# Down stage of an MLP: operand splits tied to a later product, a second output buffer, the last two jobs added to x1 on chip

## The chip, the cores and the metric

The kernel runs on one core of a Trainium2 chip. The metric is the device time of one execution in microseconds (us), the median of several runs. PE does the matmuls, ACT, DVE and POOL do elementwise work, SP issues most of the DMA transfers, POOL some.

## The reference, cut to what matters

One layer (a gated linear recurrence, a sparse attention, their merge and output projection), then an MLP with squared ReLU and a final norm, over 1024 prompt tokens and 32 sample tokens (1056 in all), in float32. The model width is 1024, the MLP's is 4096. The change is in the MLP's second half and in what follows it; all before that stays as it is.

```python
def _rmsnorm(x, g):
    xf = x.astype(jnp.float32)
    y = xf * lax.rsqrt(jnp.mean(xf * xf, axis=-1, keepdims=True) + EPS) * g.astype(jnp.float32)
    return y.astype(x.dtype)
...
def _layer(x, s0, attend, lb, w_in, hg_norm, w_a, w_b, w_o, norm1, norm2, w_up, w_down):
...
    m = jax.nn.sigmoid(ga) * y_a + jax.nn.sigmoid(gb) * y_b
    x = x + m @ w_o
    h2 = _rmsnorm(x, norm2)
    x = x + jnp.square(jax.nn.relu(h2 @ w_up)) @ w_down
    return x, s_new, ak, av, ik
...
    y_prompt = _rmsnorm(xp, norm_f)
    y_sample = _rmsnorm(xs, norm_f)
```

## The kernel before, in words

Tokens lie along the free axis, 1056 of them in two halves of 528 (TH). Both matrix products of the MLP are done as a scheme that needs seven products for eight blocks, P1 to P7, the operands of which are sums and differences of blocks. Every product runs in three passes, high part times high part and twice high times low, so each operand is split into a rounded half, o[:, 0], and a remainder, o[:, 1].

The work is a list of 32 jobs, JOBS. Jobs 0 to 15 are "up" jobs (h2 @ w_up, squared ReLU); 14 of them (NPAIR) leave seven operands each in DRAM (hc_d, by combos and the rows near L1433), and the last two leave their hidden rows in hid_d. Jobs 16 to 31 are "down" jobs (times w_down) for four rounds r and four output columns m, each over k = 2, 3 or 4 pairs of hidden rows: k is 2, 3, 4, 4 in the first round, 4 in the second and third, and 4, 3, 2, 2 in the last. A product is two halves (c = 0, 1) of k times 3 matmuls of 128x264. SEVEN is the order of all products: P2, P6, P5, P7 of a job, P1 of the next, then P4 and P3. The scheduler that places instructions on the engines' queues may still move a ready instruction ahead; an engine then works through its queue in that order.

OPS holds four slots of seven operands each (tiles h2a, h2b, h2P). An operand of a new pair is loaded by SP (op_load, L1348) into the remainder half after the last product that reads the slot's old content. op_split then casts it on ACT (L1352) and subtracts on DVE (L1353). It is written two products after the load (late_ops). The new operand is read by the same product of the next job, seven products after the load. TAKE says which job's products load which pair: 14 pairs, 98 operands, in 10 of the jobs 15 to 27, four of these with two pairs.

After a product its PSUM result is evacuated: P1, P6 and P7 by ACT's copies uu (L1398), P4 of a down job by ACT (L1406), P2, P7 and P3 by DVE's adds into hd (L1400, L1402, L1408). The weights of coming products are summed by DVE (L1290) and split on ACT and DVE (L1302, L1303). hd[j] has two rows: e = 0 comes from y0, a ring of two buffers, and e = 1 from y1, a ring of one. After P4 and P3 of a down job POOL accumulates hd into x1_d in DRAM (L1440). After each of the last four jobs the two finished rows of x1 are read back (L1447). HD, the hidden rows of the last two up jobs, is loaded (L1451) and split (L1454, L1455). Then last_w loads four weight pieces through one buffer (L1373) and splits them (L1375, L1376), and down() multiplies them with HD over three chunks of tokens (pd, L156 to L158), adds to x1 on DVE (L1497), and final() transposes (yT, L1476), normalizes and stores.

## Time and profile before

| what | value |
|---|---|
| median of 3 runs | 1807.02 us (1801.29 to 1813.28) |
| the profiled execution | 1804.69 us, its span 1803.0 us |
| PE busy in the span | 1718.2 us (95%) |
| DVE, ACT, POOL busy | 1222.6, 867.4, 216.7 us |
| up jobs end, down jobs begin | at about 1400 us |
| last stage (pd, yT) begins | at about 1714 us |

The profiled execution lies 2.3 us under the median, and 1.7 us of it are outside of the span. A busy share is an average over the whole span; the rows further down are of single stretches.

### The profile page before, as it was taken

To read this page: it belongs to the slowest core of one execution; us is meant where nothing else is said; L and a number is where in the kernel's file an instruction comes from. 1 tells how busy PE (TensorE), PEld (TensorE's weight loads), DVE (VectorE), ACT (ScalarE), POOL (GpSimd) and SP (SyncE) were. 2 spreads that over 40 slices of the span, in tenths; PEclk is the share of its full clock that TensorE was granted. 3 is DMA by queue.
4 is the path that set the end of the run, shared out by engine and by line. 5 is a ranking of instruction groups with operands and counts; after the bars stand their busy time and mean duration, and the time that the engine had idled before them with its cause. 6 is when DMAs were issued, how large, how long until landed. Compare 5 with 4: busy or idle time off the path is not lost.

```text
span 1803.0 us, 30879 instructions
## 1 busy us (share of the span) xinstructions
PE 1718.2 (95%) x11980; PEld 1656.2 (92%) x11980; DVE 1222.6 (68%) x2767; ACT 867.4 (48%) x1645; POOL 216.7 (12%) x244
## 2 busy tenths in 40 slices
PE   6999999999999999979999999999999999999887
PEld 6999999999999998877899998999999899999867
DVE  7275585745799897965747569777677866566535
ACT  6456465334578833234724455444344644444412
POOL 1100000023000015740100230000000000000110
PEclk9999999999999999999999999999999999999998
DMA  5411111231223234552543243444334877676763
GB/s 167 132 49 48 49 56 48 61 94 34 84 68 96 77 95 130 172 180 66 162 143 108 95 132 99 145 151 160 132 132 156 275 178 182 174 185 166 171 155 115
DMA packets 162706, 221.92 MB, mean 123 GB/s; under 512 B 12096, under 2 KB 117856, under 8 KB 162560
## 3 DMA queue, kind: packets, MB, share of 16 engines
q1 hardware_dynamic: 137472, 148.60, 26.4%
q0 software_dynamic: 18032, 62.18, 13.4%
q10 hardware_dynamic: 7056, 9.18, 1.4%
q8 instruction: 94, 1.54, 0.4%
q14 instruction: 52, 0.43, 0.1%
HBM read 140.31 MB, written 76.77 MB: 120 GB/s over the span
## 4 chain that ended last, share of the span: by engine, by line
PE 38%; DMA 9%; issue 8%; DVE 4%; ACT 3%; POOL 2%; DVEq 0%; SPq 0%; POOLq 0%; ACTq 0%
PE pua L1336 13%; PE puc L1336 7%; PE pub L1336 3%; DMA qb<-q_d 2%; PE po L158 2%; PE po L157 2%; PE po L156 2%; DMA h2a<-hc_d 2%; DMA wdr<-in_w_down_dram 1%; POOL qb L924 1%; DMA h2b<-hc_d 1%; DMA wbsg<-sg_d 1%; DVE pr L923 1%; PE wbp L156 1%; PE wbp L157 1%
## 5 line engine op out<-in xcount | busy, mean ns | idle before, releaser
L1336 PE MATMUL pua<-h2P,wP 128*128 128x264 f32 x1248 | 196.1, 285 | 3.5 <-ACT uu L1398 3.1
L1336 PE MATMUL pua<-h2a,wP 128*128 128x264 f32 x960 | 161.7, 287 | 13.6 <-ACT uu L1398 10.6
L1336 PEld LDWEIGHTS pua<-h2P,wP 128*128 128x128 f32 x1248 | 170.4, 189 | 4.5 <-ACT uu L1398 4.0
L1336 PEld LDWEIGHTS pua<-h2a,wP 128*128 128x128 f32 x960 | 134.6, 189 | 18.9 <-ACT uu L1398 14.8
L1398 ACT COPY uu<-pua 128x264 f32<-128x264 f32 x192 | 72.0, 378 | 133.5 <-PE pua L1336 127.4
L156 PE MATMUL wgt<-hh,wgth 128*128 128x352 f32 x384 | 126.1, 328 | 0.0
L158 PE MATMUL wgt<-hh,wgtl 128*128 128x352 f32 x384 | 125.1, 326 | 0.0
L157 PE MATMUL wgt<-hl,wgth 128*128 128x352 f32 x384 | 124.6, 324 | 0.0
L1336 PE MATMUL pua<-h2b,wP 128*128 128x264 f32 x672 | 118.4, 285 | 0.0
L1336 PE MATMUL puc<-h2P,wP 128*128 128x264 f32 x720 | 111.0, 284 | 0.6 <-DVE hd L1402 0.6
L1440 POOL DMA_DIRECT2D x_d<-hd x32 | 27.9, 873 | 612.6 <-ACT wP L1302 359.5
L1336 PEld LDWEIGHTS puc<-h2P,wP 128*128 128x128 f32 x720 | 97.1, 188 | 0.8 <-DVE hd L1402 0.8
L777 ACT ACTIVATE jkA<-sc,bstg 128x1024 bf16<-128x1024 bf16 (+5 forms) x93 | 87.1, 936 | 21.3 <-DVE bstg L796 6.0
L1336 PEld LDWEIGHTS pua<-h2b,wP 128*128 128x128 f32 x672 | 96.8, 189 | 0.1
L772 DVE TENSOR_SCALAR_CACHE_REDUCE jkD<-sc,bstg 128x768 bf16<-128x768 f32 (+3 forms) x96 | 84.4, 879 | 0.9
L1303 DVE TENSOR_TENSOR wP<-w1r,wP 128x512 fp32r<-128x512 f32 (+2 forms) x96 | 62.8, 655 | 28.8 <-ACT wP L1302 28.0
L1302 ACT CAST wP<-w1r 128x512 fp32r<-128x512 f32 (+2 forms) x96 | 57.0, 595 | 46.7 <-PE puc L1336 28.1
L156 PEld LDWEIGHTS wgt<-hh,wgth 128*128 128x128 f32 x384 | 72.2, 188 | 2.0 <-issue 1.0
L157 PEld LDWEIGHTS wgt<-hl,wgth 128*128 128x128 f32 x384 | 72.2, 188 | 1.2 <-issue 0.5
L158 PEld LDWEIGHTS wgt<-hh,wgtl 128*128 128x128 f32 x384 | 72.2, 188 | 1.2 <-issue 0.6
L1336 PE MATMUL puc<-h2a,wP 128*128 128x264 f32 x384 | 70.6, 286 | 0.9 <-DVE hd L1408 0.9
L158 PE MATMUL po<-mh,wol 128*128 128x352 f32 x192 | 62.2, 324 | 0.0
(788 smaller groups left out, 5071.2 us busy)
## 6 DMA issues: line engine op xcount, KB each, us to landing
x_d<-hd POOLq DMA_DIRECT2D x32, 528.0 KB
hc_d<-hd SPq DMA_DIRECT2D x56, 264.0 KB, 2.8
h2P<-hc_d SPq DMA_DIRECT2D x45, 264.0 KB, 3.7
sg_d<-gst ACTq DMA_DIRECT2D x48, 176.0 KB, 2.0
h2a<-hc_d SPq DMA_DIRECT2D x32, 264.0 KB, 2.8
wgtr<-in_w_in_dram SPq DMA_DIRECT2D x16, 512.0 KB, 3.9
qb<-q_d POOLq DMA_DIRECT2D x16, 512.0 KB
w1r<-in_w_up_dram SPq DMA_DIRECT2D x16, 512.0 KB, 3.9
```

What stands on the lines that cost most here:

```text
L156: nc.tensor.matmul(ps, wh, xh, start=(k == 0), stop=False)
L157: nc.tensor.matmul(ps, wh, xl, start=False, stop=False)
L158: nc.tensor.matmul(ps, wl, xh, start=False, stop=(k == n - 1))
L772: nc.vector.tensor_scalar(jkD[:, 0, :L], SC[i], s if isinstance(s, float) else s[:, a:a + 1], 0.0, op0=op, op1=ALU.add, accum_out=out[:, a ...
L777: nc.scalar.activation(jkA[:, 0, :(i + 1) * 128], src(i), AF.Sign, bias=thr[:, a:a + 1], accum_out=cnt[:, a:a + 1])
L923: nc.vector.tensor_tensor(pr, kp[:, 0:1, :].to_broadcast([128, 2, 512]), qb, op=ALU.mult)
L924: nc.gpsimd.tensor_tensor(qb, kp[:, 1:2, :].to_broadcast([128, 2, 512]), qb, op=ALU.mult)
L1302: nc.scalar.copy(w[:, 0, :n], src)
L1303: nc.vector.tensor_tensor(w[:, 1, :n], src, w[:, 0, :n].bitcast(F32), op=ALU.subtract)
L1336: nc.tensor.matmul(ps, w[:, a, k], x[:, b, sl], start=(q in "P1P2P5" and k == n_ == 0), stop=(k == k1 - k0 - 1 and n_ == 2), skip_group_ch ...
L1398: nc.scalar.copy(uu[c][:, {"P1": u1, "P6": 1, "P7": 2}[q]], ps)
L1440: nc.gpsimd.dma_start(x1_d[2 * i + e], hd[j][e], accum_op=ALU.add)
```

## The change

It edits the loop over the products and op_split in five ways. The cast of a split becomes an ACTIVATE scaled by hold, a column of ones that a small TENSOR_SCALAR (ones_after) makes from the output of the product at which the split is written. The split is written four products after its load (five where the fourth is a P5, so that P4's and P3's come together at a P7). The tile tt, free after the 14th up job, becomes a second buffer of y1 until job NJ-3's P3. The jobs NJ-2 and NJ-1 add hd to x1 on chip with DVE; for that the x1 rows 4 to 7 are read by SP and 0 and 1 by POOL after job NJ-4, and 2 and 3 after NJ-3. And the splits of HD come after P3 of job NJ-2, four products later than before, tied in the same way by a column from DVE.

```diff
@@ -1349,7 +1349,7 @@
 
     def op_split(p, q):
         o = OPS[p % 4, q]
-        nc.scalar.copy(o[:, 0], o[:, 1].bitcast(F32))
+        nc.scalar.activation(o[:, 0], o[:, 1].bitcast(F32), AF.Copy, scale=hold)
         nc.vector.tensor_tensor(o[:, 1], o[:, 1].bitcast(F32), o[:, 0].bitcast(F32), op=ALU.subtract)
 
     def combos(i):
@@ -1384,6 +1384,13 @@
         rb_chunk(prb[:, c, :CH], slice(c * CH, (c + 1) * CH))
     LO, HI = slice(0, TH), slice(TH, T)
     late_ops = collections.defaultdict(list)
+    hold = None
+
+    def ones_after(eng, src):
+
+        one = sm.tile([128, 1], F32, name="one", tag="one", bufs=4)
+        eng.tensor_scalar(one, src, 1.0, 1.0, op0=ALU.max, op1=ALU.min)
+        return one
     for g, (j, q) in enumerate(SEVEN):
         kind, i, k0, k1 = JOBS[j]
         if q == "P2":
@@ -1417,12 +1424,15 @@
             if p + 2 < NJ:
                 w_raw(p + 2, h)
 
+        if g in late_ops:
+            hold = ones_after(nc.gpsimd, uu[1][:, {"P1": u1, "P6": 1, "P7": 2}[q], 0:1] if q in ("P1", "P6", "P7") else
+                              hd[j][{"P2": 0, "P4": 1, "P3": 0}[q]][:, (T if q == "P3" else TH) - 1:][:, :1])
         for p, q_ in late_ops.pop(g, ()):
             op_split(p, q_)
         for p in range(NPAIR):
             if TAKE[p] == j:
                 op_load(p, q)
-                late_ops[g + 2].append((p, q))
+                late_ops[g + 4 + (SEVEN[g + 4][1] == "P5")].append((p, q))
         if kind == "up":
             if q in ("P2", "P7", "P4", "P3"):
                 e, sl = {"P2": (0, LO), "P7": (1, HI), "P4": (1, LO), "P3": (0, HI)}[q]
@@ -1433,25 +1443,39 @@
                     nc.sync.dma_start(hc_d[i, ORDER.index({"P2": "P1", "P7": "P3", "P4": "P2"}[q])], hd[j][e][:, sl])
             if q == "P3" and i < NPAIR:
                 combos(i)
+            if (i, q) == (NPAIR - 1, "P3"):
+                U.put(tt)
+                y1.ids.append(U.free.pop())
             if (i, q) == (NU - 1, "P3"):
-                U.put(sqs, tt)
+                U.put(sqs)
+        elif j >= NJ - 2:
+
+            if q in ("P2", "P7", "P4", "P3"):
+                e, sl = {"P2": (0, LO), "P7": (1, HI), "P4": (1, LO), "P3": (0, HI)}[q]
+                x1 = X1[2 * i + e]
+                nc.vector.tensor_tensor(x1[:, sl], x1[:, sl], hd[j][e][:, sl], op=ALU.add)
         elif q in ("P4", "P3"):
             e = int(q == "P4")
             nc.gpsimd.dma_start(x1_d[2 * i + e], hd[j][e], accum_op=ALU.add)
 
             if j >= NJ - 4 and q == "P3":
+                back = range(2 * i, 2 * i + 2)
                 if j == NJ - 4:
                     U.put(*(OPS[2, q_] for q_ in ORDER))
-                for e in range(2):
-                    X1[2 * i + e] = U.get([128, T], F32, f"x1_{2 * i + e}")
-                    nc.gpsimd.dma_start(X1[2 * i + e], x1_d[2 * i + e])
+                    back = (4, 5, 6, 7, 0, 1)
+                for m in back:
+                    X1[m] = U.get([128, T], F32, f"x1_{m}")
+                    (nc.sync if m >= 4 else nc.gpsimd).dma_start(X1[m], x1_d[m])
                 if j == NJ - 3:
                     HD = [tuple(h2b[:, 4 * a + e].rearrange("p a t -> p (a t)") for a in range(2)) for e in range(4)]
                     for e in range(4):
                         nc.sync.dma_start(HD[e][1].bitcast(F32), hid_d[e])
-        if g == len(SEVEN) - 11:
+                    U.free.append(y1.ids.pop())
+                    y1.i = 0
+        if g == len(SEVEN) - 7:
+            hold = ones_after(nc.vector, hd[j][0][:, T - 1:T])
             for hi, lo in HD:
-                nc.scalar.copy(hi, lo.bitcast(F32))
+                nc.scalar.activation(hi, lo.bitcast(F32), AF.Copy, scale=hold)
                 nc.vector.tensor_tensor(lo, lo.bitcast(F32), hi.bitcast(F32), op=ALU.subtract)
         if g == len(SEVEN) - 6:
             r0.close()
```

On ACT, where the last two operands of the pair loaded during job 21 are split, P4's and P3's: h2b is that pair's slot, wP a split weight, pua the PSUM of P1, P6, P7 and P4, hd1 the second output row. Before:

```order
L1352 CAST h2b_10251<-h2b_10251 128x528 [waits DMAHW2_49]
L1398 COPY uu_10292<-pua_15456 128x264 [waits DVE_49,PE_49]
L1406 COPY hd1_15317<-pua_15215 128x264 [waits PE_49]
L1302 CAST wP1_15516<-w0r_15245 128x512
L1398 COPY uu_10293<-pua_15456 128x264 [waits DVE_49,PE_49]
L1302 CAST wP2_15618<-w1r_15350 128x512 [waits DMAHW7_49,Activation_49]
L1352 CAST h2b_10251<-h2b_10251 128x528 [waits DMAHW4_49]
L1302 CAST wP6_15650<-ws_10294 128x512 [waits PE_49,Activation_49]
L1398 COPY uu_10292<-pua_15686 128x264 [waits PE_49]
L1398 COPY uu_10292<-pua_15456 128x264 [waits PE_49]
```

Now, at the same two operands (one is the column of ones):

```order
L1302 CAST wP2_15686<-w1r_15402 128x512 [waits DMAHW6_49,PE_49,Activation_49]
L1405 COPY uu_10293<-pua_15758 128x264 [waits PE_49]
L1302 CAST wP5_15748<-ws_10294 128x512 [waits DVE_49]
L1405 COPY uu_10293<-pua_15514 128x264 [waits PE_49]
L1302 CAST wP6_15716<-ws_10294 128x512
L1302 CAST wP3_15882<-w1r_15402 128x512 [waits DVE_49,PE_49,Activation_49]
L1405 COPY uu_10292<-pua_15514 128x264 [waits PE_49]
L1405 COPY uu_10293<-pua_15514 128x264 [waits PE_49]
L1302 CAST wP7_15785<-w0r_15291 128x512
L1352 ACTIVATE h2b_10251<-h2b_10251,one_15752 128x528 [waits DMAHW3_49,Pool_49]
L1352 ACTIVATE h2b_10251<-h2b_10251,one_15752 128x528 [waits DMAHW1_49]
L1413 COPY hd1_15621<-pua_15514 128x264 [waits DMASW4_49,PE_49]
```

Both splits now stand behind the copies of P7 and wait for the column as well as the load. Before, they stood some rows apart, the second ahead of three copies uu, and waited for the load alone.

On PE, at P4 of a job whose P4 takes operands of two new pairs (h2a and h2P4 in the wP4 rows), the order before, from P4's first half on:

```order
L1336 MATMUL pua_14964<-h2P4_10007,wP4_15063 128x264 [waits Activation_49]
L1336 MATMUL pua_14964<-h2P4_10007,wP4_15063 128x264 x2
L1336 MATMUL pua_14964<-h2b_10251,wP4_15063 128x264 x3
L1336 MATMUL pua_14964<-h2a_9339,wP4_15063 128x264 x3
L1336 MATMUL pua_14964<-h2P4_9766,wP4_15063 128x264 x3
L1336 MATMUL puc_15148<-h2P3_10008,wP3_15101 128x264 [waits DVE_49]
L1336 MATMUL puc_15148<-h2P3_10008,wP3_15101 128x264 x2
```

Now, from six matmuls behind P7's last on:

```order
L1336 MATMUL pua_15261<-h2b_10251,wP1_15059 128x264 [waits Activation_49]
L1336 MATMUL pua_15261<-h2b_10251,wP1_15059 128x264 x2
L1336 MATMUL pua_15261<-h2a_9339,wP1_15059 128x264 x6
L1336 MATMUL pua_15261<-h2P1_10002,wP1_15059 128x264 x3
L1336 MATMUL pua_14994<-h2P4_10007,wP4_15097 128x264 [waits Activation_49]
L1336 MATMUL pua_14994<-h2P4_10007,wP4_15097 128x264 x2
L1336 MATMUL pua_14994<-h2b_10251,wP4_15097 128x264 x3
L1336 MATMUL puc_15188<-h2P3_10008,wP3_15139 128x264 [waits DVE_49]
L1336 MATMUL puc_15188<-h2P3_10008,wP3_15139 128x264 x2
L1336 MATMUL puc_15188<-h2b_10251,wP3_15139 128x264 x3
L1336 MATMUL pua_14994<-h2a_9339,wP4_15097 128x264 [waits Activation_49]
L1336 MATMUL pua_14994<-h2a_9339,wP4_15097 128x264 [waits DVE_49]
```

P4's first half is begun with the two old operands, products P1 and P3 run before and behind that, and the first matmul with a new operand (wP4 with h2a) waits for ACT, the one after it for DVE. 30 matmuls lie between P7's last and it. Before, all four operands of P4 were read in a row.

On POOL, in job 23, which takes two pairs, and the start of job 24 (x1_d is x1 in DRAM), the queue before held the accumulating transfers alone; now:

```order
L1392 TENSOR_SCALAR one_15920<-uu_10293 128x1 [waits Activation_49,Pool_49]
L1392 TENSOR_SCALAR one_16026<-uu_10293 128x1 [waits Activation_49,Pool_49]
L1459 DMA x1_d_9335<-hd0_15852 128x1056 [waits DMASW2_49,DVE_49]
L1392 TENSOR_SCALAR one_16062<-hd1_15853 128x1 [waits Activation_49,Pool_49]
L1459 DMA x1_d_9335<-hd1_15853 128x1056 [waits DMASW3_49]
L1392 TENSOR_SCALAR one_16100<-hd0_15852 128x1 [waits Pool_49]
L1392 TENSOR_SCALAR one_16145<-hd0_16109 128x1 [waits DVE_49,Pool_49]
L1392 TENSOR_SCALAR one_16182<-uu_10293 128x1 [waits Activation_49,Pool_49]
```

Each column of ones (L1392) waits for an evacuation by ACT or DVE, and the transfers stand between them in the same queue.

## Rows read from the trace of the kernel before

**Rows 1.** Four stretches: length, busy time of each engine, granted clock, DMA share, GB/s.

```profile
1080.00:1400.00 320.00, 316.93 (x2576) 314.48 (x2575) 241.62 (x452) 141.65 (x284) 3.49 (x1) 1.00 0.42 141
1400.00:1436.00 36.00, 32.50 (x253) 31.03 (x252) 31.80 (x63) 25.77 (x58) 1.83 (x2) 1.00 0.85 290
1436.00:1700.00 264.00, 251.31 (x2025) 248.69 (x2024) 157.32 (x283) 122.37 (x258) 21.82 (x26) 0.99 0.69 174
1700.00:1803.00 103.00, 80.97 (x540) 73.85 (x538) 48.94 (x130) 28.25 (x78) 9.16 (x13) 0.92 0.53 148
```

**Rows 2.** What PE waited for, 1400 to 1803 us: total, times, longest.

```profile
PE pua L1336 <- ACT uu L1398: 11.7, 14, 2.0
PE yT L1476 <- DVE x L1497: 7.8, 2, 7.0
PE puc L1336 <- DVE hd L1402: 3.0, 2, 2.4
PE pd L156 <- DVE x L1497: 2.6, 2, 2.0
PE pua L1336 <- ACT wP L1302: 2.2, 2, 1.3
```

**Rows 3.** What ACT waited for at the operand cast, 1395 to 1803 us.

```profile
ACT h2b L1352 <- DMA h2b<-hc_d: 26.2, 11, 5.5
ACT h2a L1352 <- DMA h2a<-hc_d: 24.2, 16, 4.3
ACT h2P L1352 <- DMA h2P<-hc_d: 19.0, 13, 4.7
```

**Rows 4.** Timelines of SP, ACT, PE: start, duration, operation, idle time before.

```profile
1535.38 0.46 SPq L1348 DMA_DIRECT2D h2b<-hc_d  x1
...
1545.49 0.63 ACT L1352 CAST h2b<-h2b 128x528 fp32r<-128x528 f32 x1 [5.46 <-DMA h2b<-hc_d]
...
1546.97 1.18 PE L1336 MATMUL pua<-h2a,wP 128*128 128x264 f32 x6 [2.04 <-ACT uu L1398]
```

**Rows 5.** What DVE waited for, 1400 to 1803 us; then POOL's timeline.

```profile
DVE x L1497 <- DMA x<-x_d: 18.2, 3, 11.9
DVE hd L1402 <- DMA x_d<-hd: 14.0, 4, 5.4
...
1761.01 0.54 POOL L1447 DMA_DIRECT2D x<-x_d  x1 [7.24 <-DMA x_d<-hd]
```

**Rows 6.** Two stretches of the end, columns as in the first group.

```profile
1725.00:1750.00 25.00, 22.95 (x118) 19.26 (x117) 6.38 (x10) 3.60 (x7) 1.99 (x3) 0.93 0.58 137
1750.00:1775.00 25.00, 16.67 (x112) 15.59 (x111) 8.28 (x27) 4.17 (x15) 2.53 (x4) 0.86 0.48 125
```

**Rows 7.** Groups by line and shape: ns min/median/max, first and last start.

```profile
L1352 ACT CAST h2P<-h2P x45: 627/634/641, 1394.5 to 1676.7; 128x528 fp32r<-128x528 f32 x45
L1353 DVE TENSOR_TENSOR h2P<-h2P x45: 698/707/714, 1395.1 to 1677.3; 128x528 fp32r<-128x528 f32 x45
L1186 ACT CAST h2P<-x x10: 397/408/414, 1036.4 to 1060.6; 128x264 fp32r<-128x264 f32 x10
L1254 ACT ACTIVATE h<-x,g x4: 501/502/517, 1074.1 to 1080.9; 128x264 f32<-128x264 f32 x4
L1246 POOL TENSOR_TENSOR sqs<-sqs,sq x21: 937/1133/3488, 1001.4 to 1080.7; 128x352 f32<-128x352 f32 x21
```

**Rows 8.** ACT's timeline: the first and last cast of the last weights.

```profile
1713.01 1.05 ACT L1375 CAST wdh<-wdr 128x1024 fp32r<-128x1024 f32 x1 [0.69 <-DMA wdr<-in_w_down_dram]
...
1740.55 1.05 ACT L1375 CAST wdh<-wdr 128x1024 fp32r<-128x1024 f32 x1 [7.97 <-DMA wdr<-in_w_down_dram]
```

**Rows 9.** POOL's timeline, then DVE's, around 1081 us, ahead of the up jobs.

```profile
1080.71 3.49 POOL L1246 TENSOR_TENSOR sqs<-sqs,sq 128x352 f32<-128x352 f32 x1 [4.70 <-ACT sq L1245]
...
1082.95 0.43 DVE L1200 TENSOR_TENSOR tb<-h,ta 128x264 f32<-128x264 f32 x1
1084.23 0.43 DVE L1198 TENSOR_TENSOR ta<-x 128x264 f32<-128x264 f32 x1 [0.84 <-POOL sqs L1246]
```

## The prediction

> **What bounds the kernel now.** I read the table of stretches first [rows 1]. From 1080 to 1400 us, the up jobs, PE is busy 316.93 of 320.00 us at full clock: nothing is to be had there, and 2576 matmuls in that time give 0.123 us for one. What the change touches comes after 1400 us. In the transition to the down jobs (1400 to 1436) PE lacks 36.00 - 32.50 = 3.5 us while DVE is busy 31.80, which is 88%; in the other down jobs (1436 to 1700) it lacks 12.7 us; in the last stretch (1700 to 1803) 22.0 us, of which some 10 follow the last matmul and stay.
>
> The list of what PE waited for after 1400 us [rows 2] sums to 27.3 us. The largest is a wait for ACT's copies uu, 11.7 us in 14 pieces. ACT is not busy then: its own list [rows 3] says that it stood 26.2 + 24.2 + 19.0 = 69.4 us at the line of the operand cast (L1352), waiting for the DMA that loads the operand. ACT works in order, so a product's evacuation behind such a cast waits too. One instance in full [rows 4]: an operand's load is issued at 1535.38 and lands 10 us later; ACT stands 5.46 us for it, casts it at 1545.49, then a weight, then copies uu, and PE goes on at 1546.97 after 2.04 us of nothing. Nine such gaps lie between 1480 and 1676 us.
>
> Two more causes. DVE's add into hd (L1402) waited 14.0 us, 4 times, for the accumulating DMA that still read the only buffer of the second output row [rows 5]; PE lost 3.0 us by it [rows 2]. And at the end DVE's add into x1 waited 18.2 us for x1 to come back from DRAM [rows 5], since the last row is accumulated there and read back: POOL's last read is issued at 1761.01, after 7.24 us of waiting for the accumulating transfer [rows 5]. PE lost 7.8 + 2.6 us at yT and pd [rows 2], and after these gaps the granted clock fell to 0.93 and 0.86 of the full 2.4 GHz [rows 6], so that part of the matmuls ran at 1.2 GHz.
>
> **The change, part by part.** *The later split.* A split comes 4 products after its load and not 2 (5 where the fourth is P5), and its cast reads a number made from that product's output, so that it cannot be put earlier. At k = 4 a product is 24 x 0.123 = 2.95 us, so four are 11.8 us against the 10 us of that load [rows 4], and the two more are 5.9 us against the 5.5 us of the longest wait [rows 3]. So at k = 4 all the DMA waits should be gone from ACT; at k = 3 and 2 (jobs 17 and 16) the two products are 4.4 and 2.95 us, and some remain. Removed: of the waits for uu those behind the transition (between 1436 and 1700 PE lacks 12.7 us in all, 3.0 of them for hd, so 9.7), and of the two for a weight cast the longer, 1.3 (there ACT had been standing at the splits of the hidden rows, which move too). With the 3.0 for hd, which the second buffer of y1 removes, this is 9.7 + 1.3 + 3.0 = **14.0 us**.
>
> *What the tie costs.* Added are 60 small TENSOR_SCALARs on POOL (and one on DVE) and a scaled ACTIVATE in place of each of 98 casts. The scaled form took 502 ns where the cast took 408 ns at 128x264 [rows 7]; the +0.094 us carried over to 128x528 (634 ns) is 98 x 0.094 = 9.2 us of ACT. ACT is busy 122.37 of 264 us [rows 1], and the idle time covers it. The time of one small POOL instruction isn't in the trace; its bounds are nothing (it is covered) and the 0.937 us of the smallest POOL tensor instruction [rows 7]. I take 0.2, since it has one element per partition and not 352. The new wait sits on ACT, at the split; behind it are queued the weight casts and the uu copies, and PE waits for those and for the new operand itself. The spare time differs by product. Most operands are used two products after their split. P4's is used one product after it (both P4's and P3's are split at P7), and the compiled order brings the next P2 forward as well, so there some 30 to 34 matmuls, 3.7 to 4.2 us, remain. Against that stands the chain: uu copy 0.4, POOL 0.2, a weight cast that may lie between 0.6, one or two ACTIVATEs 0.6 to 1.4, DVE's subtract 0.7 to 1.4 (the last two by [rows 7]): 2.5 to 4.0 us. There are 10 jobs that take operands, so 20 such places. The cost is 0 us when all are covered; at 1.0 us each it would be 20. I take 0.2 us each, **4 us**, nearer to zero since 3.2, the chain's middle, is under the spare time.
>
> In the transition the splits get no benefit: job 16 has k = 2, DVE is nearly full [rows 1], four operands (P4's and P3's of two pairs) are split at one P7, and P1 behind it has only 18 matmuls (2.2 us). Bounds: 0 and 2 us more than the 3.5 of before; I take **1.5 us**.
>
> *The last two jobs on chip.* DVE adds hd to x1 in 8 instructions of 128x528, some 0.7 us each by the subtract of that shape [rows 7], 5.7 us in jobs where DVE is less than half busy (48.94 of 103.00 us [rows 1]); nobody waits for them but the last stage, far behind. The last four accumulating transfers, which with the reads behind them end the chain in DRAM, are gone; x1 rows 4 to 7 are read when their last accumulation, a round earlier, is long done, and rows 0 to 3 still behind their own, but two jobs and more ahead of pd. So the waits of yT and pd for x1 go: 7.8 + 2.6 = **10.4 us** [rows 2]. The clock's part: 0.07 of 22.95 and 0.14 of 16.67 us of PE in the two low stretches [rows 6] is 1.6 + 2.3 = 3.9 us at most, as part of the low clock falls on idle time; I take **2.9 us** back.
>
> What is late next? The last weights. One buffer serves four loads, and their casts start from 1713.01 to 1740.55, 9.2 us apart, the last after 7.97 us of waiting for its load [rows 8]. With the stalls gone PE would come to the fourth pair some 4 us before it is ready at that pace (an estimate: the spacing is set by buffer and load, while PE's way there loses the two shorter of its waits at x1, 2.6 us, and the low clock's first 1.6). The loads may go faster, since accumulations and read-backs no longer run beside them. The four splits of the hidden rows now come just ahead of the first pd: by twice the shorter rows [rows 7] 1.3 and 1.4 us for each, four in a row on ACT and DVE, so PE may wait 1.4 us for the first. Bounds: 0 and 4 + 1.4 = 5.4 us; I take **1.5 us**, since the loads' way is freer.
>
> **Sum.** 1804.7 (the profiled execution) - 14.0 + 4 + 1.5 - 10.4 - 2.9 + 1.5 = **1784.4 us**. The median before is 1807.0, 2.3 above that execution; with the profiled one inside the runs' spread I add only 0.6 of it and forecast 1785.
>
> *A rule against it.* The pair of rows [rows 9] shows a POOL instruction that started at 1080.71 and took 3.49 us instead of 0.94: DVE worked from one two-input subtract into the next until 1083.38 and then itself waited 0.84 us for POOL. The Trainium skill, SBUF — State Buffer, section "SBUF: two separate sides", says that VectorE and GpSimd share a pair of ports as an exclusive lock for a whole instruction when VectorE has two SBUF inputs and GpSimd reads SBUF; by that rule, and the trace agrees with it, each of the small POOL instructions can be kept waiting by a run of DVE subtracts. By the forecast's 0.2 us for such an instruction the sum is 1784; by the rule it can go as far as rival 2's 1829.
>
> **The rivals.** *1. The stalls come back in part (0.17).* If the 20 tight places lose 0.7 us each and not 0.2, that is 10 us more: 1795, within 1%. For it: the chain's upper end, 4.0 us, equals the spare time, and DVE runs at 60% in 1436 to 1700 [rows 1]. Against: the lists show ACT idle most of the time.
>
> *2. The tie is the new wait, and it is slower (0.1).* The small POOL instruction waits for a run of DVE subtracts, at worst 3.49 - 0.94 = 2.55 us [rows 9], and ACT stands at the split with the uu copies behind it, just as it stood for the DMA. It is in force at every split that PE waits for. If each of the 20 places loses 2.0 us and the 40 looser ones 0.2, that is 48 in place of 4: 1829. Without any such stall the sum is 1780, so it makes the kernel slower than before from 27 us of them on, 1.3 us at each of the 20 places, and by over 1% from 45. A run of DVE subtracts that long is seen just ahead of the up jobs, so I hold it unlikely; DVE's 88% makes the transition the next likely place [rows 1].
>
> *3. The end gives only half (0.08).* SP now fetches four x1 rows between operand and weight loads, 2.1 MB more beside loads in a stretch where the DMA engines are 69% busy [rows 1], so that w0r and w1r of the last two jobs land late, and the fourth weight keeps its old pace: 7 us of the 13.3 are lost, 1792, within 1%.
>
> *4. It doesn't do what it says (0.04).* The loads land still later than 4 products and ACT stands as before; only y1 and the end are gained: 1804.7 - 3.0 - 11.8 = 1790.
>
> **How the numbers follow.** The forecast, 1785, has 0.61; its own range is 1774 (every tie covered, the weights in time, the transition relieved too) to 1793 (0.5 us lost at each tight place). A change under 1%, 18 us, can't be told from none here, as the three runs of before span 12 us. Faster by over 1% means under 1789: 0.56 of the forecast's 0.61, and 0.03 from the better ends of rivals 1, 3 and 4. Slower by over 1%, above 1825, is 0.08 of the second rival's 0.1. The rest, 0.33, lies within 1%. The range reaches from 1773 to 1803: it takes in rivals 1, 3 and 4 and leaves out the second and a sum of several.
>
> **What would show it.** Right: ACT's waits for h2a, h2b and h2P from hc_d fall from 69.4 to under 20 us, PE's for uu from 11.7 to under 6; no wait of L1402's successor for the accumulating DMA; none of yT or pd for x1 of over 1 us, the clock at 1.00 to about 1775. The second rival would show as ACT idle at the split because of POOL, and small POOL instructions of 1 us and more. The forecast is wrong if PE's waits for h2 operands (on ACT or DVE at a split) come to over 10 us, or if the last stage waits for wdh.

## The result, and the profile after

The changed kernel takes 1786.06 us (median of 4 runs, 1783.03 to 1791.67), the kernel before in the same set 1810.15 (median of 4). The ratio worked out from the single runs is 0.9874, with a 95% interval of 0.9833 to 0.9914; the two medians alone give 0.9867. The profiled execution took 1783.03 us, its span 1781.3. The forecast was 1785.

The same table of stretches as in [rows 1], the columns are the same, of the changed kernel:

```profile
1080.00:1400.00 320.00, 317.26 (x2583) 315.15 (x2582) 237.82 (x444) 137.99 (x276) 2.09 (x1) 1.00 0.43 143
1400.00:1436.00 36.00, 32.16 (x241) 29.88 (x240) 28.94 (x57) 24.37 (x49) 5.32 (x13) 1.00 0.81 268
1436.00:1700.00 264.00, 260.36 (x2093) 256.19 (x2092) 168.82 (x305) 137.34 (x278) 40.77 (x77) 1.00 0.71 188
1700.00:1781.00 81.00, 67.74 (x463) 61.77 (x461) 49.38 (x125) 26.10 (x68) 1.63 (x3) 0.95 0.33 112
```

The up jobs are as before. From 1436 to 1700 us PE now lacks 264.00 - 260.36 = 3.6 us where it lacked 12.7, in the transition 3.8 where it lacked 3.5 (more on that further down), and in the last stretch 13.3 of 81 us where it lacked 22.0 of 103. ACT did not become less busy, it became more so (137.34 us after 122.37).

What PE waited for from 1400 us on (total, times, longest), the first eight rows, answering to [rows 2]:

```profile
PE pua L1336 <- ACT uu L1405: 3.0, 7, 0.5
PE pua L1336 <- ACT hd L1413: 1.5, 1, 1.5
PE pua L1336 <- DVE h2a L1353: 1.1, 1, 1.1
PE puc L1336 <- ACT h2a L1352: 0.9, 1, 0.9
PE puc L1336 <- DVE hd L1409: 0.8, 1, 0.8
PE pub L1336 <- DVE wP L1303: 0.8, 1, 0.8
PE pd L156 <- ACT h2b L1478: 0.8, 1, 0.8
PE pd L157 <- DVE h2b L1479: 0.6, 1, 0.6
```

The whole list sums to 10.7 us, against 28.4 before (the five rows of [rows 2], which the prediction took for the list, are 27.3 of it). The waits for uu fell from 11.7 to 3.0 us and none is above 0.5; those at yT are gone and those at pd are 1.4. New, and small, are waits for the operands themselves (h2a, from ACT or DVE). ACT's waits at the split, which were 69.4 us for DMA in [rows 3], are now for POOL's column alone:

```profile
ACT h2a L1352 <- POOL one L1392: 2.4, 6, 1.0
ACT h2P L1352 <- POOL one L1392: 1.8, 4, 0.5
ACT h2b L1352 <- POOL one L1392: 1.2, 3, 0.5
```

They sum to 5.4 us in 13 pieces; the loads have landed each time. In the end the clock holds (compare [rows 6]: 0.93 and 0.86):

```profile
1725.00:1750.00 25.00, 25.00 (x152) 22.22 (x151) 12.14 (x30) 4.14 (x13) 0.53 (x1) 1.00 0.17 61
1750.00:1775.00 25.00, 21.35 (x180) 20.78 (x178) 17.18 (x64) 10.05 (x35) 0.00 (x0) 0.97 0.29 113
```

A whole span also holds what lies ahead of the MLP, which the change doesn't touch. To take that out, the time of the MLP and the end is the span less the start of the first matmul of L1336. That start is the smallest "first" of the line's groups; the row of before and then that of the changed kernel (columns as in [rows 7]):

```profile
L1336 PE MATMUL pua<-h2a,wP x960: 278/284/422, 1077.4 to 1749.1; 128*128 128x264 f32 x192
```

```profile
L1336 PE MATMUL pua<-h2a,wP x960: 278/284/393, 1075.3 to 1726.1; 128*128 128x264 f32 x192
```

So 1803.0 - 1077.4 = 725.6 us before and 1781.3 - 1075.3 = 706.0 after: 19.6 us less. This difference, "the MLP part" from here on, is given of every run below beside the timed ratio. It is read from one trace of each kernel, and the trace is of one execution: of the slowest of those timed in e2_y1 and e6_y1x1, of the fastest or one of the fastest three in the changed kernel (both times), e3_x1, e4_untied and e7_tied2. The two traces of the kernel before differ by 6.9 us in it, those of the changed kernel by 0.8, so single differences of a few us say little, and the times stand beside them.

| run | median us | ratio to before, 95% | first L1336 | span | MLP part |
|---|---|---|---|---|---|
| before | 1807.02 | | 1077.4 | 1803.0 | 725.6 |
| before_again | 1813.28 (one run) | | 1079.1 | 1811.6 | 732.5 |
| changed | 1786.06 | 0.9874 (0.9833 to 0.9914) | 1075.3 | 1781.3 | 706.0 |
| after_again | 1781.59 | 0.9881 (0.9851 to 0.9911) | 1071.6 | 1778.4 | 706.8 |
| e1_splits | 1796.53 | 0.9953 (0.9928 to 0.9978) | 1078.0 | 1796.7 | 718.7 |
| e2_y1 | 1796.26 | 0.9940 (0.9917 to 0.9963) | 1076.8 | 1802.1 | 725.3 |
| e3_x1 | 1799.91 | 0.9953 (0.9922 to 0.9984) | 1071.3 | 1784.8 | 713.5 |
| e4_untied | 1789.65 | 0.9920 (0.9892 to 0.9947) | 1070.7 | 1785.5 | 714.8 |
| e5_pool5 | 1823.67 | 1.0106 (1.0066 to 1.0146) | 1073.8 | 1821.3 | 747.5 |
| e6_y1x1 | 1793.27 | 0.9928 (0.9902 to 0.9955) | 1076.3 | 1794.0 | 717.7 |
| e7_tied2 | 1789.72 | 0.9903 (0.9869 to 0.9937) | 1077.3 | 1784.2 | 706.9 |
| e8_hd11 | 1791.79 (one run) | | 1085.3 | 1790.1 | 704.8 |
| e9_one_act | 1794.48 | 0.9921 (0.9892 to 0.9950) | 1074.2 | 1786.7 | 712.5 |
| e10_best | 1791.38 | 0.9915 (0.9883 to 0.9947) | 1079.0 | 1790.7 | 711.7 |

### The profile page after: what moved, and what is told of

It is laid out like the page before. It is cut to its first block, busy times and chain, and to the rows that moved or that the text cites. A ratio compares the mean times of both kernels' runs of the same rounds, so it can differ in the third digit from the quotient of the medians.

```text
span 1781.3 us, 31007 instructions
## 1 busy us (share of the span) xinstructions
PE 1713.2 (96%) x11980; PEld 1650.2 (93%) x11980; DVE 1229.4 (69%) x2776; ACT 877.3 (49%) x1645; POOL 231.9 (13%) x296
## 5 line engine op out<-in xcount | busy, mean ns | idle before, releaser
L1336 PE MATMUL pua<-h2P,wP 128*128 128x264 f32 x1248 | 198.8, 285 | 1.1 <-ACT uu L1405 0.9
L1336 PEld LDWEIGHTS pua<-h2P,wP 128*128 128x128 f32 x1248 | 170.7, 188 | 2.0 <-ACT uu L1405 1.7
L1336 PE MATMUL pua<-h2a,wP 128*128 128x264 f32 x960 | 161.2, 287 | 6.4 <-ACT uu L1405 3.2
L1336 PEld LDWEIGHTS pua<-h2a,wP 128*128 128x128 f32 x960 | 134.2, 188 | 11.1 <-ACT uu L1405 5.8
L1336 PE MATMUL pua<-h2b,wP 128*128 128x264 f32 x672 | 119.9, 285 | 1.0 <-ACT uu L1405 0.9
L1336 PE MATMUL puc<-h2P,wP 128*128 128x264 f32 x720 | 113.8, 285 | 0.0
L1336 PEld LDWEIGHTS pua<-h2b,wP 128*128 128x128 f32 x672 | 97.3, 188 | 1.8 <-ACT uu L1405 1.4
L1336 PEld LDWEIGHTS puc<-h2P,wP 128*128 128x128 f32 x720 | 98.1, 188 | 0.4 <-DVE h2P L1353 0.2
L1336 PE MATMUL puc<-h2a,wP 128*128 128x264 f32 x384 | 72.7, 288 | 2.9 <-ACT h2a L1352 0.9
L1392 POOL TENSOR_SCALAR one<-uu 128x1 f32<-128x1 f32 x30 | 7.7, 257 | 492.5 <-ACT uu L1405 492.5
L1409 DVE TENSOR_TENSOR hd<-puc,uu 128x264 f32<-128x264 f32 x64 | 27.6, 431 | 56.7 <-ACT uu L1405 55.9
```

The source lines that it names most:

```text
L1336: nc.tensor.matmul(ps, w[:, a, k], x[:, b, sl], start=(q in "P1P2P5" and k == n_ == 0), stop=(k == k1 - k0 - 1 and n_ == 2), skip_group_ch ...
L1392: eng.tensor_scalar(one, src, 1.0, 1.0, op0=ALU.max, op1=ALU.min)
L1409: nc.vector.tensor_tensor(hd[j][1][:, s2], bank(j, "P5", c), uu[c][:, 2], op=ALU.add)
```

## The experiments

**One part alone: e1_splits, e2_y1, e3_x1.** Each is the kernel before with one of the three parts. e1_splits has op_split, ones_after, hold and this line of the diff:

```diff
-                late_ops[g + 2].append((p, q))
+                late_ops[g + 4 + (SEVEN[g + 4][1] == "P5")].append((p, q))
```

> The kernel before with the later, tied splits alone (y1 keeps one buffer, the last two jobs go through DRAM). My theory: ACT no longer stands for the operand loads (its waits for hc_d loads fall from 69.4 to under 5 us), PE's lack between 1436 and 1700 us falls from 12.7 to about 6 (the 3.0 us at hd stay or grow, since y1 is still held by the accumulating DMA), and the end stays as before: 1797 us or 8 us under the kernel before. Rival (the gain is that of the lighter DMA and of the second buffer, the splits only move the wait to the column of ones): lack of 11 us or more, under 2 us faster.

The MLP part fell by 6.9 us, which is no more than the two traces of before differ by, but the ratio of 0.9953 (8.5 us) says the same. PE's lack between 1436 and 1700 fell to 5.2 us. PE's waits, three of the rows:

```profile
PE pua L1336 <- ACT uu L1405: 4.9, 8, 1.9
PE puc L1336 <- DVE hd L1409: 1.9, 2, 1.3
PE yT L1486 <- DVE x L1507: 6.7, 1, 6.7
```

The waits for uu fell and that for x1 at yT stayed, as my theory had it.

e2_y1 has the second buffer alone:

```diff
-                U.put(sqs, tt)
+            if (i, q) == (NPAIR - 1, "P3"):
+                U.put(tt)
+                y1.ids.append(U.free.pop())
```

> The kernel before with the second buffer of y1 alone. My theory: only the waits for the accumulating DMA go, PE's 3.0 us at hd become 0, its waits for uu stay at 10 us or more, and the time moves by 2 to 3 us, which can't be told from none. Rival (the second buffer frees the order and carries most of the down stage's gain): the lack between 1436 and 1700 us falls below 7 us.

PE's waits in its trace, the two rows that matter:

```profile
PE pua L1336 <- ACT uu L1398: 16.6, 13, 3.0
PE puc L1336 <- DVE hd L1402: 0.2, 1, 0.2
```

The wait at hd went from 3.0 to 0.2 us, but the waits for uu were 16.6 us and the MLP part is that of before. That is the first theory's picture. The times say something else: a ratio of 0.9940 is 10.8 us, more than the 2 to 3 us expected. The trace is of the slowest of this kernel's ten runs (1803.86 us), so it can't show where the other nine were faster. What it does show is a gain that I had not expected, in the transition; it is set out further down.

e3_x1 adds the last two jobs to x1 on chip and reads x1 early, with the splits of the hidden rows where they were:

```diff
+        elif j >= NJ - 2:
...
+                nc.vector.tensor_tensor(x1[:, sl], x1[:, sl], hd[j][e][:, sl], op=ALU.add)
...
+                    back = (4, 5, 6, 7, 0, 1)
```

> The kernel before with the last two jobs added to x1 on chip and the earlier reads of x1 alone (the splits of the hidden rows stay where they were). My theory: the 10.4 us at yT and pd go with some 3 us of low clock, 12 to 14 us in all, 1793 or so, and the lack between 1436 and 1700 stays at 11 to 14 us. Rival (the lighter DMA traffic is what counts): the operand loads land sooner as well and the lack between 1436 and 1700 falls below 8 us.

The MLP part fell by 12.1 us, inside the 12 to 14 expected, but this trace is of the second fastest of ten runs (1786.47 us, where the median is 1799.91), and the ratio of 0.9953 is 8.5 us, less than expected. PE has no wait at yT or pd, and the clock at the end holds:

```profile
1725.00:1750.00 25.00, 25.00 (x153) 22.29 (x152) 11.61 (x29) 5.29 (x15) 0.53 (x1) 1.00 0.13 43
1750.00:1775.00 25.00, 24.84 (x207) 24.27 (x205) 18.56 (x60) 8.19 (x28) 0.00 (x0) 1.00 0.34 132
```

The lack between 1436 and 1700 us stayed at 13.3 us (12.7 before), so the lighter DMA traffic did not help the operand loads. Part by part the MLP part fell by 6.9 + 0.3 + 12.1 = 19.3 us, and by 19.6 with all together. That the two agree is luck: beside the second trace of before the sum is 13.8 + 7.2 + 19.0 = 40.0 us, and 26.5 together.

**The tie or the delay: e4_untied, e6_y1x1, e7_tied2.** e4_untied is the changed kernel with plain casts, still written four products after the load, and no columns:

```diff
-        nc.scalar.activation(o[:, 0], o[:, 1].bitcast(F32), AF.Copy, scale=hold)
+        nc.scalar.copy(o[:, 0], o[:, 1].bitcast(F32))
```

> The changed kernel with the splits written four products after the load, but as plain casts without the column of ones, so that the scheduler may put them earlier again. My theory (the place in the queue counts, and without the tie the place is lost): ACT's waits for hc_d loads are back at 40 us or more, PE's for uu at 8 or more, 7 to 10 us above the changed kernel. Rival (the delay in the program is enough and the column only costs): as the changed kernel or up to 3 us faster.

Without the tie the delay does not bring the gain: the MLP part is 8.8 us above the changed kernel's. PE's waits for uu are 15.2 us in all, and ACT's waits for the loads are back:

```profile
ACT h2a L1352 <- DMA h2a<-hc_d: 32.9, 18, 7.7
ACT h2b L1352 <- DMA h2b<-hc_d: 21.8, 11, 4.1
ACT h2P L1352 <- DMA h2P<-hc_d: 19.3, 14, 4.8
```

They sum to 74.0 us: the casts are in ACT's queue ahead of their loads' landing again, as the scheduler is free to put them. e6_y1x1 leaves out the split part altogether:

```diff
-                late_ops[g + 4 + (SEVEN[g + 4][1] == "P5")].append((p, q))
+                late_ops[g + 2].append((p, q))
```

> The changed kernel without its split part: plain casts two products after the load, as in the kernel before; the second buffer of y1 and the additions to x1 on chip stay. My theory: the tied split is worth 6 to 10 us on top of the other two, so 6 to 10 us above the changed kernel beside it, with ACT's waits for hc_d loads at 60 us or more. Rival (the second buffer alone gave 10 us in its median, so that it and the tie remove the same waits): 3 us or less above the changed kernel.

It stands 10.9 us above after_again in the MLP part, and by the ratios of one set, 0.9928 and 0.9881, 8.5 us. PE's largest wait in it:

```profile
PE pua L1336 <- ACT uu L1405: 17.3, 11, 6.2
```

So the tied split is worth some 9 to 11 us on top of the other parts. Beside e4_untied, 714.8 us, it also shows that the delay without the tie is worth 2.9 us at most. e7_tied2 keeps the tie and takes the delay back:

```diff
-                late_ops[g + 4 + (SEVEN[g + 4][1] == "P5")].append((p, q))
+                late_ops[g + 2 + (SEVEN[g + 2][1] == "P5")].append((p, q))
```

> The changed kernel with the tied splits two products after their load (three where the second is a P5) in place of four. My theory (loads take up to 10 us, two products of 24 matmuls 5.9): the place in ACT's queue is right but too early, ACT stands for hc_d loads again for 40 us or more, PE loses 8 us or more by it, 1789 us or more. Rival (the fixed place behind the copies is what counts, the delay is not): ACT's stand still costs PE nothing, within 3 us of the changed kernel, and better in the transition since the operands come earlier.

Here my theory was right about the place and wrong about the amount. ACT's waits for the loads:

```profile
ACT h2P L1352 <- DMA h2P<-hc_d: 5.2, 3, 2.4
ACT h2b L1352 <- DMA h2b<-hc_d: 5.1, 2, 2.7
ACT h2a L1352 <- DMA h2a<-hc_d: 2.9, 1, 2.9
```

They are 13.2 us and not 40. My 40 came from taking the one load of [rows 4], 10 us, for all: of the 50 loads whose landing the trace of before records, the median is 3.6 us and 10.1 is the longest. But where a load is late, the old stall is back with the tie in place. The last of ACT's tied splits before a copy uu, then PE (columns as in [rows 4]):

```profile
1501.32 0.73 ACT L1352 ACTIVATE h2P<-h2P,one 128x528 fp32r<-128x528 f32 x1 [2.41 <-DMA h2P<-hc_d]
1502.37 1.03 PE L1336 MATMUL pua<-h2P,wP 128*128 128x264 f32 x3 [5.03 <-ACT uu L1405]
```

ACT stood 2.85 us at another tied split just before it, so that PE waited 5.03 us for the copy behind the two. In all PE's waits from 1400 us on are 13.5 us, against 10.7 in the changed kernel. Against that the operands come earlier: PE's waits for them are 0.5 us, against 3.2. The MLP part, 706.9 us, is that of the changed kernel, and the ratios, 0.9903 and 0.9874 or 0.9881, have intervals that overlap. So most of the gain comes with the fixed place behind the product's evacuations (e6_y1x1 to e7_tied2, 10.8 us in the MLP part; the times, 0.9928 and 0.9903, can't tell these two apart). The two more products remove the rest of the waits for the loads and give as much back elsewhere.

**The price of the tie: e5_pool5, e9_one_act.** e5_pool5 makes each column in five POOL instructions, one reading the other's output:

```diff
-        one = sm.tile([128, 1], F32, name="one", tag="one", bufs=4)
-        eng.tensor_scalar(one, src, 1.0, 1.0, op0=ALU.max, op1=ALU.min)
+        n = 5 if eng is nc.gpsimd else 1
+        for n_ in range(n):
+            tag, bufs = ("one", 4) if n_ == n - 1 else ("onx", 2)
+            one = sm.tile([128, 1], F32, name=tag, tag=tag, bufs=bufs)
+            eng.tensor_scalar(one, src, 1.0, 1.0, op0=ALU.max, op1=ALU.min)
+            src = one
```

> The changed kernel with the column of ones made in five POOL instructions behind one another in place of one, so that each of the 60 columns comes 0.8 to 1.0 us later, more where DVE holds POOL up. The theory of the forecast (20 tight places, the chain at 2.5 to 4.0 us against 3.7 to 4.2 us of spare time): about half of the delay shows at the tight places and none elsewhere, PE loses 8 to 12 us more for operands at a split, 8 to 12 us slower. Rival (each of the 60 splits holds ACT and with it the next copies): 30 us slower or more. The other way (the spare time is larger than I counted): under 4 us slower.

The kernel became 41 us slower than the changed one (MLP part 747.5 after 706.0 and 706.8) and slower than before. The delay is larger than I had planned. An added instruction takes 0.21 us at the median, so four of them are 0.85 us; but many take longer. The instructions of the columns alone, in the changed kernel and in this one (the length of the stretch, busy time of DVE and of POOL, clock, DMA share, GB/s):

```profile
1395.00:1720.00 325.00, 0.15 (x1) 23.34 (x60) 1.00 0.72 198
1395.00:1720.00 325.00, 0.00 (x0) 111.15 (x300) 0.98 0.64 173
```

A column of the changed kernel takes 0.41 us on average. Here, from the start of the first instruction to the end of the fifth, it takes 2.30 us on average and 1.58 at the least, so it comes some 1.9 us later and not 0.85.

ACT's waits at the split, of this kernel:

```profile
ACT h2a L1352 <- POOL one L1395: 26.8, 22, 2.2
ACT h2P L1352 <- POOL one L1395: 25.4, 17, 2.5
ACT h2b L1352 <- POOL one L1395: 16.2, 14, 2.3
```

That is 68.4 us in 53 pieces, as long as the waits for DMA in [rows 3] were. Yet PE's waits for uu are 7.6 us, not far above the 3.0 of the changed kernel. What grew is its waits for the operands themselves, of which these are the two largest:

```profile
PE pua L1336 <- ACT h2a L1352: 3.7, 6, 1.2
PE pua L1336 <- ACT h2P L1352: 3.5, 4, 1.6
```

All waits of this kind (for h2a, h2b and h2P, from ACT or DVE, at L1336) sum to 21.8 us in 40 pieces, against 3.2 in 5. PE's listed gaps grew from 10.7 to 34 us in all; of the other 17 us the low clock accounts for some 7 (the first 40 us from 1400 on have 0.91), and the rest isn't resolved. e9_one_act makes the columns on ACT:

```diff
+        if eng is nc.scalar:
+            eng.activation(one, src, AF.Copy, bias=1.0, scale=0.0)
...
-            hold = ones_after(nc.gpsimd, uu[1]
+            hold = ones_after(nc.scalar, uu[1]
```

> The changed kernel with the 60 columns of ones made on ACT itself (an ACTIVATE of one element per partition) in place of POOL. By the run with five POOL instructions a delay of a column shows nearly in full; so a shorter way to the column should gain. My theory: ACT has no wait for POOL (5.4 us now), the operand waits of PE in the transition (3.0 us) fall to 2 or less, 1 to 3 us faster, which the trace shows and the times hardly. Rival (60 more instructions on ACT, some 0.2 us each, in front of the copies): 1 to 5 us slower.

The rival's size was about right: the MLP part is 712.5 us, 6 us more. Its reason, later copies, is not what the trace shows. ACT's 60 instructions take 0.2 us each, the waits for POOL are gone, PE's waits for the copies uu grew from 3.0 to 3.9 us only, and the larger part is new waits for DVE's weight split:

```profile
PE pua L1336 <- ACT uu L1408: 3.9, 8, 0.9
PE pua L1336 <- DVE wP L1303: 3.8, 2, 2.0
```

Why DVE comes late with wP there stays open.

**The end: e8_hd11, e10_best.** e8_hd11 has the splits of the hidden rows where they were, as plain casts:

```diff
-        if g == len(SEVEN) - 7:
-            hold = ones_after(nc.vector, hd[j][0][:, T - 1:T])
+        if g == len(SEVEN) - 11:
```

> The changed kernel with the splits of the hidden rows where they were, four products earlier and as plain casts; all else as changed. My theory (a term of 1.3 us: there ACT stands for the loads of the hidden rows with a weight cast behind it): a gap of 1 us or more on PE at a weight cast or a copy in the last two jobs, and the two gaps ahead of pd, 0.75 and 0.56, gone: 0 to 2 us slower in the trace. Rival: nothing waits there any more, 1 us faster.

Of the two gaps ahead of pd, 0.75 and 0.56 us, one of 0.37 is left, for a weight. The gap that my theory had at a copy came: the last split of the hidden rows stands 2.44 us for its load, a copy uu stands behind it, and PE waits for that copy.

```profile
1713.28 1.07 ACT L1477 CAST h2b<-h2b 128x1056 fp32r<-128x1056 f32 x1 [2.44 <-DMA h2b<-hid_d]
1714.68 0.63 PE L1336 MATMUL pua<-h2a,wP 128*128 128x264 f32 x3 [1.28 <-ACT uu L1405]
```

The MLP part is all the same 704.8 us, 1.2 to 2.0 less than the changed kernel's two, which one trace can't tell from none. e10_best builds on e9_one_act:

```diff
-                    U.free.append(y1.ids.pop())
+                    spare = y1.ids.pop()
...
             r1.close()
+            U.free.append(spare)
...
-        if g == len(SEVEN) - 7:
-            hold = ones_after(nc.vector, hd[j][0][:, T - 1:T])
+        if g == len(SEVEN) - 8:
+            hold = ones_after(nc.vector, hd[j][1][:, TH - 1:TH])
```

> The run with the columns on ACT, and two edits at the end: the buffer that y1 gives back is freed behind those of the weights, so that the first wdh doesn't take it while the accumulating DMA still reads it, and the splits of the hidden rows come one product earlier. My theory: of PE's three gaps at the end (1.48 at hd, 0.75 and 0.56 at pd) 1.5 us or more go, so 2 to 4 us faster than the changed kernel in all. Rival (the cast of wdh, now free of that wait, is put earlier and stands for its load): the gap comes back at another place, 0 us.

Two of the three gaps at the end, 1.48 and 0.75 us, went, yet the MLP part is 711.7 us. The rival came true: the first cast of wdh, free of its wait for the buffer, now stands for its load with two copies uu behind it, and PE waits longer than the two gaps together.

```profile
1708.90 1.04 ACT L1375 CAST wdh<-wdr 128x1024 fp32r<-128x1024 f32 x1 [5.03 <-DMA wdr<-in_w_down_dram]
1710.27 1.03 PE L1336 MATMUL pua<-h2a,wP 128*128 128x264 f32 x3 [3.96 <-ACT uu L1408]
```

Waits for DVE's weight split are there too, 3.1 us after the 4.4 of e9_one_act. No kernel here is faster than the changed one beyond what can be told.

**Once more: after_again, before_again.** Both are the kernels unchanged.

> The changed kernel once more, on the chip of this set, for a second trace and so that the two kernels below have it beside them. My theory (its gain is in waits that it removes for good): 1783 to 1790 us and a lack of PE between 1436 and 1700 us of 3 to 6 us, as in its first trace. Rival (the first trace was a lucky one): 1790 us or more, a lack of over 8 us.

> The kernel before once more, for a second trace of it. My theory: the same waits in the same places, PE lacking 11 to 15 us between 1436 and 1700 us and 9 us or more at yT and pd. Rival (the waits for the accumulating DMA differ much between executions, and the first trace showed a small one): PE waits at hd for 6 us or more, or DVE for the accumulating DMA for 25 us or more.

The changed kernel repeats to 0.8 us in the MLP part (706.0 and 706.8), with a lack of 3.6 us between 1436 and 1700 in both traces. The kernel before doesn't repeat: 725.6 and 732.5, with a lack of 12.7 and 16.7 us between 1436 and 1700. That is more than the 11 to 15 I expected of it, and its waits at yT and pd, 7.6 us, are less than the 9. Three rows of what PE waited for in its second trace, beside [rows 2]:

```profile
PE pua L1336 <- ACT uu L1398: 19.0, 14, 3.5
PE puc L1336 <- DVE hd L1402: 2.5, 2, 2.3
PE yT L1476 <- DVE x L1497: 7.1, 1, 7.1
```

The waits for uu were 19.0 us and not 11.7; those at hd 2.5, so the accumulating DMA is not what varies. In the other kernels with untied splits the waits for uu lie between 13.7 and 17.3 us.

## Why the prediction was right

The time came out as forecast, 1786 us for 1785, and the waits that were to go went. The terms behind it did not all come out, and two of the misses cancel.

*The wait for the operand loads (14.0 us removed, 4 given back).* Of the 14.0 us, 12.7 lay in the stretch from 1436 to 1700 us; less the 4 of the tie that is 8.7, and 9.1 was measured in the first pair of traces (12.7 to 3.6 us). The split part alone gave 6.9 us in the MLP part, on top of the others 9 to 11. The mechanism, ACT standing in its queue at a cast with the copies behind it, holds. The reason given for the cure was wrong in one half. I worked out that two more products (5.9 us) outlast the longest wait (5.5 us), with one load of 10 us standing for all. e4_untied shows that four products without the tie bring little, and e7_tied2 that two products with it bring the same time as four: the forced place behind the evacuations does most of it. The two more products remove the 13.2 us that ACT still stood for loads, and the 5.03 us that PE lost by it at one place, but no time that can be told apart is won by that.

*What the tie costs (4 us).* As a size this was about right: PE's waits for operands are 3.2 us and those left at uu 3.0. As a place it was wrong, which is luck. The 4 us were to be 0.2 at each of 20 tight places, but of the 3.2 all except 0.5 lie in the transition. The chain itself is borne out better by e5_pool5 than by its expectation. A column 1.9 us later, of which half shows at 20 places, is 19 us; PE's waits for operands rose by 18.6. The whole cost was 41 us, since other waits and the clock came on top, so the chain does not give the time. Whether the 40 looser places cost anything was not sorted out by place. If the cost is linear in the delay, which two points don't show, the 19.6 us of gain would be used up at some 0.9 us more per column. It didn't come to pass since the columns are short. The rows of the changed kernel's split and its columns (columns as in [rows 7]):

```profile
L1352 ACT ACTIVATE h2P<-h2P,one x45: 719/726/747, 1410.9 to 1677.5; 128x528 fp32r<-128x528 f32 x45
L1392 POOL TENSOR_SCALAR one<-uu x30: 209/209/580, 1401.3 to 1675.4; 128x1 f32<-128x1 f32 x30
L1392 POOL TENSOR_SCALAR one<-hd x30: 204/539/1210, 1412.8 to 1662.6; 128x1 f32<-128x1 f32 x30
```

The scaled form costs 0.726 - 0.634 = 0.092 us more at 128x528, against 0.094 carried over from the smaller tile. A column takes 0.21 us at its shortest, as taken, and up to 1.2 us. What makes it long can be read from the traces: a long one mostly ends just behind a DVE TENSOR_TENSOR that takes no input from PSUM, much as [rows 9] had it for one instruction. One case of the changed kernel (columns as in [rows 4]):

```profile
1527.72 0.70 DVE L1353 TENSOR_TENSOR h2P<-h2P 128x528 fp32r<-128x528 f32 x1
1528.03 0.46 POOL L1392 TENSOR_SCALAR one<-uu 128x1 f32<-128x1 f32 x1 [2.37 <-ACT uu L1405]
```

DVE's subtract ends at 1528.42 us, the column at 1528.49. Of the 60 columns 27 start while neither such a TENSOR_TENSOR nor the issue of an accumulating DMA is under way; their median is 0.21 us and the longest 0.25. The 16 that start inside such a TENSOR_TENSOR, with no issue beside them, have a median of 0.46, and 14 of them end 0.06 to 0.08 us behind it. In e5_pool5 these are 108 of 300 instructions, with a median of 0.64 us, and 107 of them end so. The 15 with both have a median of 0.73, so the issue may add to it.

*The transition (1.5 us).* It went from 3.5 to 3.8 us of lack. That the forecast's added 1.5 us did not show is luck, because two things cancel. In stretches of 36 us that begin 322.6 us after each kernel's first L1336, as the one from 1400 us on does in the kernel before, these are e6_y1x1 (second buffer, no tie) and then the changed kernel (columns as in [rows 1]):

```profile
1398.90:1434.90 36.00, 34.46 (x273) 33.34 (x272) 32.39 (x66) 26.19 (x59) 1.85 (x2) 1.00 0.81 284
1397.90:1433.90 36.00, 32.54 (x246) 30.48 (x245) 27.66 (x55) 23.95 (x49) 5.32 (x13) 1.00 0.80 272
```

The lack is 1.5 us without the tie and 3.5 with it. Counted the same way it is 1.3 in e2_y1 and e4_untied, which also have the second buffer and no tie; 3.5, 4.1 and 4.3 in the two traces of before and in e3_x1, which have neither; and 3.4 in e1_splits, which has the tie alone. So the second buffer wins some 2 us there, in which I had given it nothing, and the tie takes some 2 us back, near the upper bound of what I gave it. DVE's load there didn't rise as I feared (31.80 to 28.94 us busy in the stretch), but the waits are where I put them, at operands.

*hd (3.0 us).* In the trace of e2_y1 the wait is gone from the stretch from 1436 to 1700, and the transition is 2 us shorter, but the waits for uu are 4.9 us longer than in the first trace of before. Since those differ by 7.3 us between the two traces of before itself, one trace can't give the term's worth. In the changed kernel a part of the wait has moved to the other row. In its second trace DVE's add at P2 (L1407), whose row comes from y0, waits 3.12 and 4.35 us for the accumulating DMA, near 1688 and 1700 us, and PE 0.64 and 0.93 us for the add at P7 that stands behind it. What makes e2_y1 faster in the times by 10.8 us stays open. e1_splits, e2_y1 and e3_x1 together time faster (8.5 + 10.8 + 8.5 = 27.8 us, each ratio times 1807) than the change (22.8), but each of these figures is uncertain by 4 to 7 us, so the times don't show whether the parts add up.

*The end (10.4 + 2.9 - 1.5 = 11.8 us).* e3_x1 measured 12.1 us in its trace and 8.5 in the times. The waits of yT and pd for x1 went whole, the clock came back to 1.00 and 0.97, and the new cost is 1.4 us at pd, with 1.5 at a copy hd behind ACT's first cast of wdh. The fourth weight was in time. The 1.3 us that I gave to the place of the hidden rows' splits are there: with the splits back at the old place, e8_hd11 has the gap of 1.28 us at a copy. They were not a gain, since the new place costs as much at pd (0.75 and 0.56 us).

*Rivals.* 1, 3 and 4 did not occur. Of 2, the first half is so in the changed kernel: small POOL instructions wait for DVE's, and then take up to 0.64 us with no DMA issue beside them. The second half is not: ACT's waits for them are 5.4 us in all. In e5_pool5 ACT stands for POOL as long as it stood for the DMA, yet PE waits less for the copies behind it than it did before (7.6 and 11.7 us) and more for the operands, so the wait came to PE by the forecast's own chain more than by the rival's.

## What to carry to other kernels

Where an in-order engine stands at an instruction for a transfer, look at what is queued behind it: here the instruction's place in the queue counted for more than two products more between load and use. A false dependence on a later result fixes that place where a scheduler would hoist it. The two traces with it lie closer together (706.0 and 706.8 us) than the two without (725.6 and 732.5), which is too few to call it the reason. It also puts a small instruction of another engine on the path at every use: try it with a delay in that instruction, to see the margin, and measure the delay itself, which here came to 1.9 us for a planned 0.85. And take the price of a transfer from many of them, not from the longest.

## What was not expected of the hardware

The part ahead of the MLP, the same in all 14 traces but for what the scheduler may have moved, ended between 1070.7 and 1085.3 us; one and the same kernel moved by 1.7 us (before) and 3.7 us (changed). A part of this may be the granted clock: between 100 and 400 us it was 0.98 in the changed kernel's trace and 0.95 in that of e1_splits (the same stretch, columns as in [rows 1]).

```profile
100.00:400.00 300.00, 298.23 (x2038) 286.65 (x2037) 187.06 (x349) 149.71 (x248) 20.01 (x31) 0.98 0.22 60
```

```profile
100.00:400.00 300.00, 297.20 (x1998) 285.78 (x1997) 184.72 (x346) 147.01 (x243) 16.49 (x25) 0.95 0.20 57
```

So a whole span or a single time carries up to 15 us from the part ahead of the MLP, and the first start of a line behind that part is a better zero.
